# One softplus for the stick-breaking rows, softmax division on ScalarE, doubled queries in one GpSimd operation

## The chip, the core and the metric

The kernel runs on one core of one Trainium2 chip. A core has a matrix engine (TensorE, in the profile PE, with its weight loads as PEld), a vector engine (VectorE, DVE), an engine for activation functions (ScalarE, ACT), a general one (GpSimd, POOL) and one that issues transfers (SyncE, SP). Each works through its own list of instructions in order; semaphores tie the lists together. SBUF is the working memory, PSUM the memory that PE writes its results to, in banks of 128 rows by 512 fp32 columns.

The metric is device time in microseconds for one execution, as the median of several runs.

## The reference

One layer of a decoder on 1024 tokens of width 1024, in fp32: a norm, one input projection, three kinds of heads side by side, an output projection with a residual, and a squared-ReLU MLP with a residual. The change touches two of the three kinds of heads, each with six heads of width 64:

```python
def stick_breaking_attn(q, k, v):          # q, k: RMS-normed per head
    ...
    z = jnp.einsum('bhqd,bhsd->bhqs', qi, k) * scale
    mask = kpos[None, :] < qpos[:, None]
    log_1mb = jnp.where(mask, jax.nn.log_sigmoid(-z), 0.0)
    tail = lax.cumsum(log_1mb, axis=3, reverse=True) - log_1mb
    A = jnp.where(mask, jnp.exp(jnp.where(mask, jax.nn.log_sigmoid(z) + tail, 0.0)), 0.0)
    ...
def forgetting_attn(q, k, v, c):
    ...
    s = jnp.einsum('bhqd,bhsd->bhqs', qi, k) * scale + bias
    p = jax.nn.softmax(jnp.where(mask, s, NEG_BIG), axis=-1)
```

With sp(z) = ln(1 + exp(z)), the stick-breaking weight of a key is exp(z - S), where S is the sum of sp over this key and all later ones up to the query. So a row needs a softplus of each score, a running sum from the right, a subtraction and an exponential.

## The kernel before

The mixer part runs as eight units: six units m0 to m5, each with one stick-breaking head and one forgetting head, and two units of the recurrent heads (hg0, hg1), in the order m0, hg0, m1, m2, m3, hg1, m4, m5. While the core of one unit runs, the projection of the next (or, beside m5, the first part of the output projection) is laid between its steps, so that PE has matmuls whose inputs are ready. The steps are emitted by due times (`place`, with the tables SPAN and POW), and a scheduler then orders the instructions on each engine; that order is fixed when the program is built.

In `attn` a unit goes through 16 tiles of 128 queries (8 for each of its heads). A tile's keys come in one or two pieces of up to 512 columns; the widths are 128, 256, 384 or 512. That makes 12 pieces for each head and unit, 72 over the six units for each kind of head.

- `qprep` (L359) makes the queries ready, 256 at a time: POOL multiplies them by the per-token norm factor and writes them twice side by side (`qd`, L365, two operations), PE transposes them into PSUM (`qtp`, L369), ACT scales them by the gain and rounds (`qj`, L371), and DVE makes the remainder (L372). PE multiplies the pair with the keys.
- `qtile` (L375) makes the scores `z` in a PSUM bank (L396 to L399) and turns them into weights. Banks of the kind `z` are three, shared with `qtp` and some transposes.
- A stick-breaking piece (L401 to L416) is copied to SBUF by ACT (`zs`, L403). DVE takes the absolute value (L404), ACT makes exp and ln(1 + .) of it (L406, L407), DVE takes max(z, 0) (L409) and runs the scan from the right over both (L411). A subtraction (L414) runs on DVE in units 0, 2, 3, 4 and on POOL in 1 and 5, and ACT makes the last exponential (L415).
- A forgetting piece (L418 to L441) is read from PSUM by DVE, which takes off the bias and keeps the row maximum (L420); ACT makes the exponential with its row sum (L432), DVE the reciprocal of the sum (L437 or L439) and the product with it (L441).
- `back` (L444) transposes the weights on PE (L453) and evicts them (L457 on ACT, L459 on DVE); `av` (L465) multiplies them with the values (L472).

Several lines belong to helpers: L130 and L133 are the rounding and the remainder of `split`, which cuts an fp32 operand into two parts for the matmuls, and L173 to L175 are the three matmuls of `mm3`.

Per-token factors `qnr` are kept in five buffers, two of them taken by a unit. The rest of the program, from about 680 us on, is the second norm and the MLP, with one level of Strassen's scheme in each of its two products.

Of the kernel before, what the change touches and what calls it, by code (L numbers as in the profile page):

```python
# [18 lines left out]
P = 128  # L19
# [8 lines left out]
NEG = -1e30  # L28
C = 64
# [35 lines left out]
def hybrid_block(ctx, tc, x, lb_logits, norm1_g, w_in, hg_norm_g, sb_q_g, sb_k_g, fox_q_g, fox_k_g,  # L65
# [288 lines left out]
    def attn(name):  # L354
# [4 lines left out]
        def qprep(h, qq):  # L359
            half, q2 = divmod(qq, 2)  # L360
            gq = gq_fx if h else gq_sb
            ts = slice(q2 * 2, q2 * 2 + 2)
            qd = big("qd", "qd", [P, 2, 2, HD])
            for e in range(2):
                G.tensor_tensor(out=qd[:, :, e, :], in0=st["q"][half][:, ts, h, :],  # L365
                                in1=st["r"][half][:, ts, h:h + 1].broadcast_to([P, 2, HD]), op=ALU.mult)
            tp = pt("z", "qtp")[:, :256]
            for i in range(2):
                PE.transpose(out=tp[:, i * P:(i + 1) * P], in_=qd[:, i].rearrange("p e d -> p (e d)"), identity=ident)  # L369
            qj = big("qj", "qj", [P, 2, 256], F32R)  # L370
            S.activation(qj[:, 0], tp, AF.Copy, scale=gq)  # L371
            V.scalar_tensor_tensor(out=qj[:, 1], in0=tp, scalar=gq, in1=qj[:, 0], op0=ALU.mult, op1=ALU.subtract)  # L372
            cur["q", h, qq] = qj

        def qtile(h, i):  # L375
# [16 lines left out]
            for c, w in reversed(pcs):  # L392
# [7 lines left out]
                if sbk:  # L400
                    e = big("e", "sbe")[:, :w]  # L401
                    zs = big("zs", "sbz")[:, :w]
                    S.copy(zs, z)  # L403
                    V.tensor_scalar(out=e.bitcast(I32), in0=zs.bitcast(I32), scalar1=0x7fffffff, scalar2=None,  # L404
                                    op0=ALU.bitwise_and)
                    S.activation(e, e, AF.Exp, scale=-1.0)  # L406
                    S.activation(e, e, AF.Ln, bias=1.0)  # L407
                    r = big("r", "sbr")[:, :w]
                    V.tensor_scalar(out=r, in0=zs, scalar1=0.0, scalar2=None, op0=ALU.max)  # L409
                    rv = r[:, ::-1]  # L410
                    V.tensor_tensor_scan(out=rv, data0=rv, data1=e[:, ::-1], initial=0.0 if prev is None else prev,  # L411
                                         op0=ALU.add, op1=ALU.add)
# [11 lines left out]
            if not sbk:  # L424
# [15 lines left out]
                for c, w in pcs:  # L440
                    V.tensor_scalar(out=a_of[c], in0=a_of[c], scalar1=r, scalar2=None, op0=ALU.mult)  # L441
# [451 lines left out]
    V.memset(one_t, 1.0)  # L893

# [236 lines left out]
    PLACES = {"f_m": {"xo": (16, [P, 512]), "usum": (4, [P, 512]), "t1": (2, [P, 2, 512]), "ya": (3, [P, 2, 512]), "pad": (1, [P, 144])},  # L1131
# [176 lines left out]
```

## Time and profile before

| | |
|---|---|
| median of 3 runs | 1360.47 us (1359.05 to 1361.12) |
| the profiled execution | 1361.72 us |
| its span in the profile | 1360.0 us |
| PE busy | 1284.2 us, 94% |
| PE weight loads | 1064.6 us, 78% |
| DVE busy | 997.7 us, 73% |
| ACT busy | 707.4 us, 52% |
| POOL busy | 279.8 us, 21% |
| mean granted clock of PE | 0.979 of full speed |

A row of a group gives the line, the engine, the operation, the tile written and the tiles read, the shape, the count, then busy time in us and the mean of one in ns, then the time for which the engine stood idle just ahead of these instructions and what ended most of it. "(+3 forms)" says that several widths are in the group. PE's matmuls are pipelined and their ends are modelled, so a busy PE is not always PE at its peak. The chain of work that ended last is followed back from the last instruction: at each step to what released it, or to the instruction ahead of it on its engine.

### The profile page before, as it was taken

How to read it: one execution, taken by the hardware profiler on the slowest of the kernel's cores; microseconds unless marked ns; L12 is line 12 of the kernel's file. 1: busy time of each engine (PE TensorE's matmuls, PEld its weight loads, DVE VectorE, ACT ScalarE, POOL GpSimd, SP SyncE). 2: the span in 40 equal slices, each digit the busy share in tenths (PEclk: the TensorE clock that was granted, in tenths of full speed). 3: DMA queues.
4: the chain of work that ended last, by engine and by line, in shares of the span. 5: the costliest groups of instructions: out<-in, count | busy, mean ns of one | idle time of the engine just before them, and what ended most of it. 6: DMA issues, size and time to landing. Idle time of an engine off the chain costs nothing.

```text
span 1360.0 us, 19999 instructions
## 1 busy us (share of the span) xinstructions
PE 1284.2 (94%) x7200; PEld 1064.6 (78%) x7200; DVE 997.7 (73%) x1855; ACT 707.4 (52%) x1537; POOL 279.8 (21%) x342
## 2 busy tenths in 40 slices
PE   4999989989899899799897999999999899999998
PEld 4978878868688788467685888888887688888887
DVE  6758667877768668977669766666766898786865
ACT  5557344877688346765446554544454533333430
POOL 7112695432225764421100000000000000000000
PEclk9999998999999989799898999999999999999999
DMA  8200211200202020343453354344435973534322
GB/s 222 51 17 9 71 25 40 63 24 25 55 17 63 9 55 32 109 124 99 135 167 120 132 171 145 130 159 162 147 128 182 393 258 105 201 110 146 118 78 93
DMA packets 125931, 149.25 MB, mean 110 GB/s; under 512 B 46460, under 2 KB 73084, under 8 KB 125832
## 3 DMA queue, kind: packets, MB, share of 16 engines
q1 hardware_dynamic: 100464, 101.79, 24.6%
q10 hardware_dynamic: 25368, 46.17, 9.6%
q8 instruction: 57, 0.93, 0.3%
q14 instruction: 42, 0.34, 0.1%
HBM read 104.40 MB, written 43.54 MB: 109 GB/s over the span
## 4 chain that ended last, share of the span: by engine, by line
PE 75%; DVE 14%; ACT 4%; issue 2%; DMA 2%; POOL 2%; SPq 0%; ACTq 0%; POOLq 0%; DVEq 0%
PE pj L173 5%; PE pj L174 5%; PE pj L175 5%; PE av L472 3%; DVE sbr L411 3%; PE pc L1019 2%; PE pd L1018 2%; PE pc L1018 2%; PE pd L1019 2%; PE pd L1020 2%; PE pc L1199 2%; PE pc L1198 2%; PE pc L1020 2%; PE pc L1197 2%; PE pa L1018 2%
## 5 line engine op out<-in xcount | busy, mean ns | idle before, releaser
L173 PE MATMUL pj<-whi,hTh 128*128 128x384 f32 (+2 forms) x512 | 172.2, 339 | 2.2 <-ACT vg L619 1.2
L174 PE MATMUL pj<-wlo,hTh 128*128 128x384 f32 (+2 forms) x512 | 171.5, 336 | 0.0
L175 PE MATMUL pj<-whi,hTl 128*128 128x384 f32 (+2 forms) x512 | 170.9, 334 | 0.0
L130 ACT CAST fah<-ya 128x1024 fp32r<-128x1024 f32 x56 | 58.8, 1050 | 168.1 <-PE pd L1198 49.6
L173 PEld LDWEIGHTS pj<-whi,hTh 128*128 128x128 f32 x512 | 98.6, 193 | 5.9 <-ACT vg L619 1.5
L174 PEld LDWEIGHTS pj<-wlo,hTh 128*128 128x128 f32 x512 | 98.5, 192 | 2.5 <-issue 1.9
L175 PEld LDWEIGHTS pj<-whi,hTl 128*128 128x128 f32 x512 | 98.2, 192 | 2.3 <-issue 1.3
L411 DVE TENSOR_TENSOR_SCAN sbr<-sbr,sbe 128x128 f32<-128x128 f32 (+3 forms) x72 | 78.3, 1092 | 10.3 <-ACT sbe L407 9.6
L133 DVE TENSOR_TENSOR fal<-ya,fah 128x1024 fp32r<-128x1024 f32 x56 | 68.2, 1219 | 21.8 <-ACT fah L130 21.7
L365 POOL TENSOR_TENSOR qd<-qraw,qnr 128x128 f32<-128x128 f32 x96 | 47.8, 519 | 160.6 <-PE qtp L369 151.0
L472 PE MATMUL av<-at,vst 128*64 128x256 f32 x480 | 68.5, 368 | 1.6 <-ACT at L457 0.8
L133 POOL TENSOR_TENSOR wlo<-wraw,whi 128x384 fp32r<-128x384 f32 (+2 forms) x56 | 58.7, 1073 | 35.9 <-ACT whi L130 22.4
L457 ACT COPY at<-atp 128x128 f32<-128x128 f32 (+3 forms) x120 | 56.3, 479 | 10.5 <-PE atp L453 9.2
L133 DVE TENSOR_TENSOR fbl<-w2raw,fbh 128x1024 fp32r<-128x1024 f32 x48 | 58.2, 1215 | 1.6 <-ACT fbh L130 1.6
L173 PE MATMUL po<-woh,mTh 128*128 128x512 f32 x128 | 53.6, 418 | 4.8 <-DVE x L856 2.4
L397 PE MATMUL z<-kst,qj 128*128 128x512 f32 (+3 forms) x144 | 50.3, 374 | 7.1 <-DVE qj L372 7.1
L472 PEld LDWEIGHTS av<-at,vst 128*64 128x64 f32 x480 | 36.9, 137 | 25.6 <-issue 5.0
L396 PE MATMUL z<-kst,qj 128*128 128x512 f32 (+3 forms) x144 | 51.7, 384 | 4.0 <-ACT qj L371 3.6
L415 ACT ACTIVATE sbz<-sbz 128x128 f32<-128x128 f32 (+3 forms) x72 | 37.9, 529 | 30.2 <-DVE sbz L414 23.8
L432 ACT ACTIVATE fxa<-fxa,fxmn 128x512 f32<-128x512 f32 (+2 forms) x72 | 43.8, 612 | 18.8 <-DVE fxmn L427 9.8
L130 ACT CAST fbh<-w2raw 128x1024 fp32r<-128x1024 f32 x48 | 49.7, 1047 | 6.4 <-DMA w2raw<-in_w_ff_dram 5.1
L174 PE MATMUL po<-wol,mTh 128*128 128x512 f32 x128 | 52.1, 407 | 0.0
(355 smaller groups left out, 3786.9 us busy)
## 6 DMA issues: line engine op xcount, KB each, us to landing
w1raw<-in_w_ff_dram SPq DMA_DIRECT2D x32, 512.0 KB, 5.8
w2raw<-in_w_ff_dram SPq DMA_DIRECT2D x16, 1024.0 KB, 6.6
ya<-yd_s SPq DMA_DIRECT2D x32, 512.0 KB, 3.8
yd_s<-y ACTq DMA_DIRECT2D x48, 256.0 KB, 4.6
ya<-yd_a SPq DMA_DIRECT2D x24, 512.0 KB, 3.8
wraw<-in_w_in_dram SPq DMA_DIRECT2D x48, 192.0 KB, 3.3
wraw<-in_w_in_dram SPq DMA_DIRECT2D x16, 256.0 KB, 4.3
xraw<-in_x_dram SPq DMA_DIRECT2D x16, 256.0 KB, 3.4
```

The costliest lines, as they stand in the source:

```text
L130: S.copy(hi, raw)
L133: lo_eng.tensor_tensor(out=lo, in0=raw, in1=hi, op=ALU.subtract)
L173: PE.matmul(o, lhsT=lh, rhs=rh, start=start, stop=False)
L174: PE.matmul(o, lhsT=lh, rhs=rl, start=False, stop=False)
L175: PE.matmul(o, lhsT=ll, rhs=rh, start=False, stop=stop)
L396: PE.matmul(z, lhsT=qj[:, 0, qs], rhs=kst[:, :w], start=True, stop=False)
L411: V.tensor_tensor_scan(out=rv, data0=rv, data1=e[:, ::-1], initial=0.0 if prev is None else prev, op0=ALU.add, op1=ALU.add)
L457: S.copy(dst, tv)
L472: PE.matmul(o[h * HD:(h + 1) * HD, c0:], lhsT=st["v"][j // 4][:, j % 4, h, :], rhs=at[h][j // 4][:, j % 4, c0:], start=(j == 0), stop=(j = ...
L1018: PE.matmul(o, lhsT=wh[:, k], rhs=bh[:, k], start=start and k == 0, stop=False, **kw)
L1019: PE.matmul(o, lhsT=wh[:, k], rhs=bl[:, k], start=False, stop=False, **kw)
L1020: PE.matmul(o, lhsT=wl[:, k], rhs=bh[:, k], start=False, stop=k == 3, **kw)
```

## The change

```diff
+ZMAX = 40.0
...
+            q = st["q"][half][:, ts, h, :].unsqueeze(2).broadcast_to([P, 2, 2, HD])
             qd = big("qd", "qd", [P, 2, 2, HD])
-            for e in range(2):
-                G.tensor_tensor(out=qd[:, :, e, :], in0=st["q"][half][:, ts, h, :],
-                                in1=st["r"][half][:, ts, h:h + 1].broadcast_to([P, 2, HD]), op=ALU.mult)
+            if h:
+                G.tensor_tensor(out=qd, in0=q, op=ALU.mult,
+                                in1=st["r"][half][:, ts, h:h + 1].unsqueeze(3).broadcast_to([P, 2, 2, HD]))
+            else:
+                G.tensor_copy(qd, q)
...
                     zs = big("zs", "sbz")[:, :w]
-                    S.copy(zs, z)
-                    V.tensor_scalar(out=e.bitcast(I32), in0=zs.bitcast(I32), scalar1=0x7fffffff, scalar2=None,
-                                    op0=ALU.bitwise_and)
-                    S.activation(e, e, AF.Exp, scale=-1.0)
+                    V.tensor_scalar(out=zs, in0=z, scalar1=st["r"][i // 4][:, i % 4, 0:1], scalar2=ZMAX, op0=ALU.mult, op1=ALU.min)
+                    S.activation(e, zs, AF.Exp)
                     S.activation(e, e, AF.Ln, bias=1.0)
                     r = big("r", "sbr")[:, :w]
-                    V.tensor_scalar(out=r, in0=zs, scalar1=0.0, scalar2=None, op0=ALU.max)
-                    rv = r[:, ::-1]
-                    V.tensor_tensor_scan(out=rv, data0=rv, data1=e[:, ::-1], initial=0.0 if prev is None else prev,
-                                         op0=ALU.add, op1=ALU.add)
+                    V.tensor_tensor_scan(out=r[:, ::-1], data0=e[:, ::-1], data1=zero_t[:, 0:1].broadcast_to([P, w]),
+                                         initial=0.0 if prev is None else prev, op0=ALU.add, op1=ALU.add)
...
                 for c, w in pcs:
-                    V.tensor_scalar(out=a_of[c], in0=a_of[c], scalar1=r, scalar2=None, op0=ALU.mult)
+                    S.activation(a_of[c], a_of[c], AF.Copy, scale=r)
...
+    zero_t = const.tile([P, 1], F32, name="zero_t")
+    V.memset(zero_t, 0.0)
...
-    PLACES = {"f_m": {..., "pad": (1, [P, 144])},
+    PLACES = {"f_m": {..., "pad": (1, [P, 136])},
```

Four things change. The softplus is made in one branch: scores are bounded at 40, and ln(1 + exp(z)) is taken as it stands; absolute value, maximum and ACT's copy go, and the scan adds a zero that is repeated from one column. The norm factor of a stick-breaking query is no longer put into the query but into the same DVE operation that bounds the score, which reads PSUM. The division of the softmax goes from DVE to ACT. The doubled queries are written by one POOL operation, a plain copy for the stick-breaking head. A padding tile in the memory layout of the MLP is 8 columns narrower, beside the new constant of one column.

In numbers of instructions: DVE loses 144 (72 each of L404 and L409) and 72 (L441) and gains 72; ACT loses 72 copies and gains 72 products; POOL has 48 operations for queries where it had 96. PE's instructions and the transfers stay as many as they were. Since the scheduler works the whole program anew, other instructions move against each other too.

The first place is DVE's list in unit m4, at the two stick-breaking tiles with one and two pieces (`sbz` are scores, `sbe` the exponentials, `sbr` the running sums). Before:

```order
L404 TENSOR_SCALAR sbe<-sbz 128x128
L409 TENSOR_SCALAR sbr<-sbz 128x128
L404 TENSOR_SCALAR sbe<-sbz 128x512
L409 TENSOR_SCALAR sbr<-sbz 128x512
L411 SCALAR_TENSOR_TENSOR sbr<-sbr,sbe 128x128
L414 TENSOR_TENSOR sbz<-sbz,sbr 128x128
L411 SCALAR_TENSOR_TENSOR sbr<-sbr,sbe 128x512
L302 COPY vst<-pj 128x128
L414 TENSOR_TENSOR sbz<-sbz,sbr 128x512
```

And in the change, whose lines stand a little further down (its L409 is the new operation on PSUM, with `qnr` the norm factors, L413 the scan, L416 the subtraction):

```order
L409 TENSOR_SCALAR sbz<-z,qnr 128x128
L409 TENSOR_SCALAR sbz<-z,qnr 128x512
L413 SCALAR_TENSOR_TENSOR sbr<-sbe,zero_t 128x128
L416 TENSOR_TENSOR sbz<-sbz,sbr 128x128
L413 SCALAR_TENSOR_TENSOR sbr<-sbe,sbr,zero_t 128x512
L416 TENSOR_TENSOR sbz<-sbz,sbr 128x512
L409 TENSOR_SCALAR sbz<-z,qnr 128x256
```

Four operations ahead of the scans have become two; these read the bank `z` themselves, and the next piece's one stands behind two scans and two subtractions.

The second place is ACT's list in the same unit, where a forgetting tile's exponentials stand (`fxa` are its weights, `fxmn` the negated maximum, `mTh` the rounding of a part of the output projection's operand). Before:

```order
L432 ACTIVATE fxa,fxs<-fxa,fxmn 128x512
L432 ACTIVATE fxa,fxs<-fxa,fxmn 128x256
L406 ACTIVATE sbe<-sbe 128x384
L130 CAST mTh<-mraw 128x512
L406 ACTIVATE sbe<-sbe 128x512
L403 COPY sbz<-z 128x512
```

And in the change (L434 is the exponential, L443 the product with the reciprocal `fxr`, L410 and L411 the exp and ln of the softplus):

```order
L434 ACTIVATE fxa,fxs<-fxa,fxmn 128x512
L434 ACTIVATE fxa,fxs<-fxa,fxmn 128x256
L410 ACTIVATE sbe<-sbz 128x384
L138 ACTIVATE qnln<-qss,eps_t 128x16
L817 DMA mraw<-mix_m_1820 128x512
L443 ACTIVATE fxa<-fxa,fxr 128x512
L443 ACTIVATE fxa<-fxa,fxr 128x128
L131 CAST mTh<-mraw 128x512
L443 ACTIVATE fxa<-fxa,fxr 128x512
L443 ACTIVATE fxa<-fxa,fxr 128x256
L411 ACTIVATE sbe<-sbe 128x384
```

The products of two tiles now stand on ACT, ahead of the logarithm of a stick-breaking piece, and the copy from the bank has gone.

More of the change, by code (lines that the diff above doesn't have):

```diff
@@ L1129, in hybrid_block @@
     U = [None] * 4
-    PLACES = {"f_m": {"xo": (16, [P, 512]), "usum": (4, [P, 512]), "t1": (2, [P, 2, 512]), "ya": (3, [P, 2, 512]), "pad": (1, [P, 144])},
+    PLACES = {"f_m": {"xo": (16, [P, 512]), "usum": (4, [P, 512]), "t1": (2, [P, 2, 512]), "ya": (3, [P, 2, 512]), "pad": (1, [P, 136])},
               "f_hop": {"w2f": (1, [P, 2, D]), "yf": (2, [P, 2, 512]), "fof": (4, [P, 2, 512])},
```

## The prediction

> **What bounds the kernel now.** I read the page's first part, then busy time by stage (one window per unit), then the chain of work that ended last inside the stages with holes, and last the groups by line and by shape.
>
> ```profile
> span 1360.0 us, 19999 instructions
> 75.00:165.00 90.00, 86.19 (x575) 73.66 (x574) 65.67 (x157) 55.33 (x141) 27.91 (x35) 0.98 0.14 33
> 225.00:300.00 75.00, 70.99 (x445) 59.30 (x443) 62.02 (x157) 56.18 (x155) 31.20 (x36) 0.98 0.16 43
> 300.00:375.00 75.00, 70.87 (x404) 57.85 (x403) 55.03 (x125) 50.89 (x129) 17.82 (x22) 0.98 0.15 39
> 375.00:450.00 75.00, 75.00 (x539) 64.87 (x539) 52.81 (x120) 57.65 (x147) 26.66 (x31) 1.00 0.15 36
> 525.00:600.00 75.00, 62.28 (x349) 45.00 (x347) 65.76 (x143) 55.57 (x138) 30.52 (x37) 0.91 0.29 92
> 600.00:675.00 75.00, 69.05 (x357) 52.20 (x357) 50.08 (x111) 39.88 (x93) 11.60 (x12) 0.95 0.39 122
> 750.00:1360.00 610.00, 600.86 (x2623) 492.57 (x2621) 434.67 (x574) 256.94 (x357) 0.00 (x0) 1.00 0.47 159
> ```
>
> The columns are stretch, length, busy time of PE, weight loads, DVE, ACT and POOL, then the granted clock and the DMA share. From 750 us on PE is busy 600.86 of 610 us and nothing of the change runs there: that 45% of the span cannot move. The change lives in the six attention units, 75 to 675 us. There PE is full in 375 to 450 (75.00 of 75), so faster helpers gain nothing in that unit. It has holes in the others, the largest in 525 to 600: PE 62.28, weight loads only 45.00, DVE 65.76 of 75. So the question is what carries the chain in the stages with holes; the rows below are shares of 75 us, for 225, 300, 525 and 600 in turn.
>
> ```profile
> by line: DVE sbr L411 13.6%; issue 8.1%; ACT fxa L432 6.9%; PE av L472 5.7%; DVE sbe L404 4.4%; DVE fxa L420 3.9%; DMA wraw<-in_w_in_dram 3.6%; POOL qsq L311 3.5%; DVE qj L372 3.5%; DVE fxa L441 3.5%; DVE sbr L409 3.1%; PE atp L453 3.0%; AC
> by line: PE pj L173 14.8%; PE pj L174 13.8%; PE pj L175 13.7%; PE atp L453 8.2%; PE av L472 6.9%; DVE sbr L411 6.7%; DVE sbe L404 4.8%; PE z L397 4.1%; PE z L396 4.1%; DVE sbr L409 3.4%; DVE sbz L414 2.9%; DVE qsq L311 1.9%; PE qtp L369 1.8
> by line: DVE sbr L411 14.3%; DVE mTl L133 9.5%; PE av L472 7.1%; issue 6.5%; DVE sbz L414 6.2%; DVE fxa L441 5.1%; DVE sbr L409 4.4%; DVE kst L326 4.0%; PE pj L174 3.7%; DVE fxa L420 3.6%; DVE sbe L404 3.5%; PE pj L173 3.3%; PE pj L175 3.3%
> by line: PE po L173 14.0%; PE po L174 12.8%; PE po L175 12.7%; PE av L472 8.9%; PE atp L453 7.9%; DVE sbr L411 6.0%; issue 5.8%; DMA woraw<-in_w_out_dram 4.8%; DVE at L459 3.1%; DVE wol L133 2.7%; DVE fxa L420 2.6%; DVE sbr L409 2.3%; PE z
> ```
>
> The stick-breaking scan L411 leads the chain in two stages, and the three DVE operations that the change removes, L404, L409 and L441, stand on it beside the scan.
>
> **The change, part by part.**
>
> ```profile
> L404 DVE TENSOR_SCALAR sbe<-sbz 128x128 int32<-128x128 int32 (+3 forms) x72 | 32.2, 447 | 27.0 <-ACT sbz L403 26.6
> L409 DVE TENSOR_SCALAR sbr<-sbz 128x128 f32<-128x128 f32 (+3 forms) x72 | 31.2, 433 | 0.2
> L441 DVE TENSOR_SCALAR fxa<-fxa,fxr 128x512 f32<-128x512 f32 (+2 forms) x72 | 34.0, 503 | 0.9
> L403 ACT COPY sbz<-z 128x128 f32<-128x128 f32 (+3 forms) x72 | 33.6, 486 | 24.9 <-PE z L399 23.9 <-PE z L397 0.5
> L459 DVE COPY at<-atp 128x512 f32<-128x512 f32 (+3 forms) x24 | 13.2, 548 | 1.2 <-PE atp L453 1.2
> L420 DVE CUSTOM_DVE_ANT_0 fxa<-z,cb 128x128 f32<-128x128 f32 (+3 forms) x72 | 38.7, 549 | 12.3 <-PE z L399 11.7 <-PE z L397 0.2
> L372 DVE SCALAR_TENSOR_TENSOR qj<-qtp,gq_sb,qj 128x256 fp32r<-128x256 f32 x24 | 11.4, 474 | 0.8 <-ACT qj L371 0.6
> L459 DVE COPY at<-atp 128x256 f32<-128x256 f32 x4 | 1.7, 417 | 0.2 <-PE atp L453 0.2
> ```
>
> *Stick-breaking rows.* For 72 pieces ACT loses its copy L403 (33.6 us). DVE loses L404 and L409 (63.4 us) and gains one operation that reads PSUM with a per-row scalar. Its price is not in the trace. The floor is L404's 447 ns mean, as if PSUM cost nothing. L459 and L420 read PSUM at 548 and 549 ns over the same mix of widths. L372 reads PSUM with a per-row scalar too and takes 474 ns where the plain L459 copy of that width takes 417, 57 more. I take 549 + 57 = 606 ns, nearest to those rows: 43.6 us, between 32.2 and 43.6. So DVE sheds 63.4 - 43.6 = 19.8 us here, up to 31.2.
>
> ```profile
> 543.07 1.48 POOL L311 TENSOR_TENSOR qsq<-qraw 128x512 f32<-128x512 f32 x1
> 543.58 1.12 DVE L404 TENSOR_SCALAR sbe<-sbz 128x256 int32<-128x256 int32 x1
> 546.29 0.43 DVE L404 TENSOR_SCALAR sbe<-sbz 128x512 int32<-128x512 int32 x1
> 547.19 0.68 DVE L420 CUSTOM_DVE_ANT_0 fxa<-z,cb 128x512 f32<-128x512 f32 x1
> ```
>
> The saving lies in disturbed pieces. Undisturbed, L404 does 512 columns in 0.43 us and the PSUM reader L420 takes 0.68, so two for one gains little. While a POOL operation runs, L404 took 1.12 us for half the columns.
>
> The Trainium skill, "VectorE: DVE Perf Modes", section "Why PSUM operands drop a tier", speaks against this part: an fp32 operand in PSUM holds the operation to one element a cycle, where SBUF allows two. The undisturbed rows agree (0.68 against 0.43), and by them two for one saves 0.86 - 0.68 = 0.18 us a wide piece, 13 us over 72, against the 0.27 us a piece and 19.8 us that the means above, with POOL running, give; I keep the means.
>
> *The scan* keeps two operands, one now a repeated zero.
>
> ```profile
> L411 DVE TENSOR_TENSOR_SCAN sbr<-sbr,sbe 128x512 f32<-128x512 f32 x36 | 49.4, 1373 | 3.1 <-ACT sbe L407 2.9
> L411 DVE TENSOR_TENSOR_SCAN sbr<-sbr,sbe 128x128 f32<-128x128 f32 (+3 forms) x72 | 78.3, 1092 | 10.3 <-ACT sbe L407 9.6
> L588 DVE TENSOR_TENSOR_SCAN hb<-ht,ha 128x512 f32<-128x512 f32 x4 | 4.9, 1215 | 0.6 <-POOL ht L587 0.6
> ```
>
> A wide scan costs 1373 ns as now, or at best the 1215 of L588: 158/1373 of 78.3 us is 9 us, at most gained, or lost if the repeated operand were read slower. I take 0, since the order of the elements, both inputs from SBUF and the subtraction behind it stay.
>
> *Softmax division.* DVE sheds L441, 34.0 us; ACT gains 72 multiplications with a per-row scale.
>
> ```profile
> L432 ACT ACTIVATE fxa<-fxa,fxmn 128x512 f32<-128x512 f32 (+2 forms) x72 | 43.8, 612 | 18.8 <-DVE fxmn L427 9.8 <-DVE fxmn L429 8.2 <-DVE fxr L437 0.8
> L415 ACT ACTIVATE sbz<-sbz 128x128 f32<-128x128 f32 (+3 forms) x72 | 37.9, 529 | 30.2 <-DVE sbz L414 23.8 <-POOL sbz L414 5.8
> ```
>
> Same tile, same per-row pointer: 612 ns (L432), at least the 529 of L415 without one. So ACT gains 43.8 and loses 33.6: 10.2 us more, hidden in the fullest DVE stage, where ACT is busy 55.57 of 75. What stands bare is the new wait: ACT stops at each L441 in its order until DVE's reciprocal is done, and the next exponentials, evictions and casts queue behind it.
>
> The Trainium skill, "ScalarE: Activation LUTs", section "Rules for kernel authors", says to multiply on VectorE and not on ScalarE. The trace agrees on one operation alone: 612 against 503 ns. By it the sum would be that of rival 4 below.
>
> *Queries.* POOL issues 48 operations of 256 columns for 96 of 128, half of them plain copies.
>
> ```profile
> L365 POOL TENSOR_TENSOR qd<-qraw,qnr 128x128 f32<-128x128 f32 x96 | 47.8, 519 | 160.6 <-PE qtp L369 151.0 <-issue 9.6
> L675 POOL TENSOR_TENSOR hx<-hx,hf 128x256 f32<-128x256 f32 x24 | 22.4, 936 | 16.4 <-ACT hx L671 15.8
> PEld z L397 <- DVE qj L372: 9.3, 8, 2.4
> DVE sbe L404 <- ACT sbz L403: 26.6, 15, 5.0
> ```
>
> Two of 519 become one of at most 936 (L675); half a copy may halve it. POOL mostly waits here (160.6 us), so this alone is worth little: 8 waits of PE for qj, 0.1 to 0.5 us nearer each, 1 us at the low end. No DMA is added or moved.
>
> *Sum.* On the chain rows, L404 and L409 hold 3.3 + 2.3, 3.6 + 2.6, 3.3 + 2.6 and 1.7 us, 19.4 in all. The larger of the two in each stage over its mean gives 7.4 + 8.1 + 7.6 + 3.9 = 27 pieces, which come back at 606 ns: 16.4. Net -3.0. The 15 waits of DVE for the copy (last row above) lose one 486 ns step each, 7.3 us; I count half, the rest falling where PE is full or DVE has slack: -3.6. L441 holds 2.6 + 3.8 = 6.4 us, 13 pieces. Where DVE is the bound all of it goes, where the row's own delay is the bound it becomes 0.1 us longer; half and half: -2.5. Queries -1. Together **-10 us**. Behind this PE's own order is late next: PE idles 4.0, 4.1, 12.7 and 6.0 us in the four stages, so 27 us is about the most that filling them could give. I leave out 75 to 165, where PE idles 3.8 of 90.
>
> **The rivals.**
>
> ```profile
>   PEld z L396: 0.2, 1
> L414 DVE TENSOR_TENSOR sbz<-sbz,sbr 128x512 f32<-128x512 f32 x24 | 19.3, 803 | 0.3
> L404 DVE TENSOR_SCALAR sbe<-sbz 128x512 int32<-128x512 int32 (+3 forms) x13 | 6.1, 466 | 5.4 <-ACT sbz L403 5.4
> L409 DVE TENSOR_SCALAR sbr<-sbz 128x512 f32<-128x512 f32 (+3 forms) x13 | 6.4, 489 | 0.0
> L441 DVE TENSOR_SCALAR fxa<-fxa,fxr 128x512 f32<-128x512 f32 (+3 forms) x12 | 6.6, 574 | 0.2
> ```
>
> 1. *The scores' PSUM bank waits for DVE (slower).* Today ACT frees the three z banks; afterwards DVE does, in order, behind a scan and a subtraction. A PE that needs the bank then waits up to 1.373 + 0.803 = 2.18 us (L411 and L414, wide). The gain is eaten at five such waits; at seven of the 72, 15.3 - 10 = +5.3: 1367.0. For: DVE is the fullest helper in 525 to 600. Against: the forgetting heads' scores are already read from such a bank by DVE (L420), and under "who waited for it" the view of that line has one wait of PE, 0.2 us (first row). Chance 0.14.
> 2. *Hidden anyway.* PE takes over at once, as in 375 to 450, or a moved order opens as many holes as it closes: -1, 1360.7. Chance 0.14.
> 3. *DVE alone sets the stages.* The rows for 525 to 600 remove 6.1 + 6.4 + 6.6 = 19.1 us and bring back 13 x 0.606 = 7.9: -11.2 there. If 225 to 300, with a like DVE load, gives the same, -22: 1339.7. For: DVE 65.76 of 75. Against: PE idles only 4.0 us at 225. Chance 0.12.
> 4. *The division is on the delay path.* All 13 chain pieces of L441 lengthen by 0.1 us (612 - 503) instead of going: +1.4 in place of -2.5, so -6: 1355.7. For: ACT's L432, the operation just ahead, holds 6.9% of the chain at 225. Against: at 525 the chain has no ACT line among its first thirteen. Chance 0.10.
>
> **How the numbers follow.** The profiled run took 1361.72 us, span 1360.0 and 1.7 around it; the median of the runs is 1360.47, 1.25 less. Forecast: 1361.72 - 10 = 1351.7, or **1350.5** as a median, chance 0.50. The rivals' times are in the profile's terms too; less 1.25 they are 1365.8, 1359.5, 1338.5 and 1354.5. The range, 1337 to 1366, takes in all five and the cheaper scan's few microseconds on the chain. A measurement here tells about 0.2%, 2.7 us, from no change. Faster: 0.50 + 0.12 + 0.10 = 0.72; same 0.14; slower 0.14.
>
> **What would show it.** Right: DVE busy time falls by some 54 us (97.4 out, 43.6 in), ACT's rises by about 10, POOL's falls; the new line takes about 0.68 to 0.74 us for 512 columns and keeps that beside POOL; PE's idle time shrinks most in the unit of 525 to 600 and not at all in the one of 375. Wrong: PE waits for z banks whose reader is the new DVE line (rival 1); a stage as long as before with less DVE in it (rival 2); ACT idle before the multiplication, with the reciprocal as releaser, and PE's transposes waiting on it (rival 4); a scan of more than 1.4 us.

## The result, and the profile after

| | before | after |
|---|---|---|
| median of 5 runs | 1360.47 us (1355.44 to 1361.12) | 1368.95 us (1366.46 to 1371.53) |
| the profiled execution | 1361.72 us | 1366.46 us |
| its span | 1360.0 us | 1364.7 us |
| after to before | | 1.0071, 95% interval 1.0045 to 1.0096 |

The change made the kernel slower, by 8.5 us at the medians and 4.7 us between the two profiled executions. The forecast was 1350.5 us.

The page of after, its first part and its chain by engine:

```profile
span 1364.7 us, 19810 instructions
PE 1290.6 (95%) x7200; PEld 1066.1 (78%) x7200; DVE 979.0 (72%) x1712; ACT 715.6 (52%) x1537; POOL 261.5 (19%) x294
PE 83%; DVE 7%; ACT 4%; POOL 2%; issue 2%; DMA 1%; SPq 0%; ACTq 0%; POOLq 0%; DVEq 0%
```

DVE's share of the chain that ended last fell to 7%, from 14% on before's page. So the change took DVE off the chain, as it was meant to, and the kernel is slower all the same. The new operations and the scan, as groups by line (after has other line numbers: L409 is the bounded score, L413 the scan, whose second row is the pieces that carry on from another, L443 the product on ACT, L676 one step of the recurrent heads):

```profile
L409 DVE TENSOR_SCALAR sbz<-z,qnr 128x128 f32<-128x128 f32 (+3 forms) x72 | 42.6, 611 | 15.7 <-PE z L403 10.1 <-PE atp L455 4.7 <-PE z L401 0.5
L413 DVE TENSOR_TENSOR_SCAN sbr<-sbe,zero_t 128x128 f32<-128x128 f32 (+3 forms) x48 | 42.5, 894 | 14.8 <-ACT sbe L411 11.9 <-issue 1.1 <-POOL kraw L316 1.0
L413 DVE TENSOR_TENSOR_SCAN sbr<-sbe,sbr,zero_t 128x512 f32<-128x512 f32 x24 | 36.8, 1533 | 2.6 <-ACT sbe L411 2.4
L443 ACT ACTIVATE fxa<-fxa,fxr 128x512 f32<-128x512 f32 (+2 forms) x72 | 41.4, 609 | 5.8 <-DVE fxr L439 4.6 <-DVE fxr L441 1.1
L676 DVE TENSOR_TENSOR hxq<-hx,hq 64x256 f32<-64x256 f32 x24 | 29.0, 1251 | 2.7 <-PE hz L681 2.6
```

The prices were right: 611 ns for the new operation, 79.3 us for the scan (78.3 before), 609 ns for the product. The last row is not of the change: `hxq` cost 17.3 us before, with the same 24 operations. Busy time by stage, in the columns of the prediction's windows:

```profile
225.00:300.00 75.00, 72.24 (x453) 61.19 (x452) 56.26 (x126) 59.87 (x157) 26.23 (x27) 0.98 0.16 43
300.00:375.00 75.00, 74.00 (x443) 59.51 (x440) 48.22 (x112) 55.85 (x137) 15.53 (x15) 1.00 0.16 40
375.00:450.00 75.00, 73.66 (x522) 64.69 (x521) 53.39 (x97) 55.10 (x142) 31.83 (x34) 1.00 0.16 40
450.00:525.00 75.00, 62.94 (x650) 57.52 (x649) 62.00 (x103) 30.48 (x89) 41.06 (x42) 0.89 0.12 33
525.00:600.00 75.00, 64.88 (x357) 46.78 (x356) 61.23 (x124) 56.44 (x141) 29.77 (x31) 0.91 0.28 88
```

PE gained 1.25 us of busy time at 225, 3.13 at 300 and 2.60 at 525. It lost 6.64 in 450 to 525 (before's row there has PE at 69.58), the stage of the recurrent unit hg1. Milestones in the traces say the same. The last output of unit m3 is copied at 446.4 us, 5.8 earlier than before (452.2); the last of hg1 at 522.6, 2.4 later (520.2); the MLP's first matmul starts at 724.7, 3.0 later (721.7); the span ends 4.7 later. So the gain was there at 446 us, and was given back in hg1, in the last unit and in the MLP.

Where hg1 lost it, in the timeline of after (start, length, engine, line; in brackets the idle time of the engine just ahead and what ended it):

```profile
471.71 9.67 DVE L676 TENSOR_TENSOR hxq<-hx,hq 64x256 f32<-64x256 f32 x1
...
472.36 1.27 POOL L716 TENSOR_TENSOR hkd<-hkd,hf 128x512 f32<-128x512 f32 x1
473.59 1.26 POOL L725 TENSOR_TENSOR hb<-hb,hq 128x512 f32<-128x512 f32 x1
474.82 1.25 POOL L716 TENSOR_TENSOR hkd<-hkd,hf 128x512 f32<-128x512 f32 x1
476.04 1.25 POOL L725 TENSOR_TENSOR hb<-hb,hq 128x512 f32<-128x512 f32 x1
477.26 3.83 POOL L134 TENSOR_TENSOR wlo<-wraw,whi 128x384 fp32r<-128x384 f32 x4
...
481.52 1.23 PE L681 MATMUL hz<-hxq,hx 128*64 128x64 f32 x18 [8.48 <-DVE hxq L676]
```

One DVE operation, 0.42 us where it is undisturbed, took 9.67 us while POOL ran on to 481.09 without a pause; PE stood idle for 8.48 us until it was done. Two other kernels below with the same lists in hg1, x1_merge and x3_div, show 9.70 us each, so it is no chance of one execution.

### The profile page after: what moved, and what is told of

It reads as the page before. It is cut to its first block, busy times and chain, and to the rows that moved or that the text cites. A ratio compares the mean times of both kernels' runs of the same rounds, so it can differ in the third digit from the quotient of the medians.

```text
span 1364.7 us, 19810 instructions
## 1 busy us (share of the span) xinstructions
PE 1290.6 (95%) x7200; PEld 1066.1 (78%) x7200; DVE 979.0 (72%) x1712; ACT 715.6 (52%) x1537; POOL 261.5 (19%) x294
## 4 chain that ended last, share of the span: by engine, by line
PE 83%; DVE 7%; ACT 4%; POOL 2%; issue 2%; DMA 1%; SPq 0%; ACTq 0%; POOLq 0%; DVEq 0%
PE pj L174 7%; PE pj L176 6%; PE pj L175 6%; PE av L474 4%; PE atp L455 3%; PE pd L1201 2%; PE pc L1024 2%; PE pc L1023 2%; PE pc L1022 2%; PE pd L1022 2%; PE pd L1023 2%; PE pd L1024 2%; PE pc L1202 2%; PE pc L1203 2%; PE pc L1201 2%; PE pa L1022 2%
## 5 line engine op out<-in xcount | busy, mean ns | idle before, releaser
L474 PE MATMUL av<-at,vst 128*64 128x256 f32 x480 | 71.7, 383 | 2.0 <-DVE at L461 0.9
L409 DVE TENSOR_SCALAR sbz<-z,qnr 128x128 f32<-128x128 f32 (+3 forms) x72 | 42.6, 611 | 15.7 <-PE z L403 10.1
L413 DVE TENSOR_TENSOR_SCAN sbr<-sbe,zero_t 128x128 f32<-128x128 f32 (+3 forms) x48 | 42.5, 894 | 14.8 <-ACT sbe L411 11.9
L434 ACT ACTIVATE fxa<-fxa,fxmn 128x512 f32<-128x512 f32 (+2 forms) x72 | 43.8, 610 | 17.0 <-DVE fxmn L431 9.6
L1201 PE MATMUL pd<-fbh,fah 128*128 128x512 f32 x128 | 49.6, 400 | 2.2 <-ACT fbh L131 2.2
```

What stands on the lines that cost most here:

```text
L474: PE.matmul(o[h * HD:(h + 1) * HD, c0:], lhsT=st["v"][j // 4][:, j % 4, h, :], rhs=at[h][j // 4][:, j % 4, c0:], start=(j == 0), stop=(j = ...
L1201: PE.matmul(o, lhsT=lh[:, ts], rhs=rh, start=start and q == q0, stop=False, **kw)
```

## Experiments

Each experiment's ratio is to runs of before on the same chip. Three theories were set against each other: that the new **operations** cost what they save; that a **collision** and the **placement** of tiles took the gain; that the **order** that the scheduler finds anew decides.

### Placement, the collision, the tail

**x1_merge**: the change, with the zero put into the tile of ones, so that every later tile should keep before's address. In after, the new constant has moved the tiles between it and the padding; by how far is worked out from the padding, which gives up 8 columns of fp32 in exchange: 32 bytes in each row.

```diff
-    one_t = const.tile([P, 1], F32, name="one_t")
-    zero_t = const.tile([P, 1], F32, name="zero_t")
+    oz_t = const.tile([P, 4], F32, name="oz_t")
+    one_t, zero_t = oz_t[:, 0:1], oz_t[:, 1:2]
...
-    "pad": (1, [P, 136])
+    "pad": (1, [P, 144])
```

> The changed kernel with one edit: the new zero column lies in the tile of the ones, and the MLP's padding tile is 144 columns wide again, so that every later tile lies where it lay before the change. No engine's order changes. Theory (where the constant lies): the matmuls of the MLP's first product, 229.0 ns apart before and 231.9 after, go back to 229, and from 725 to 1050 us some 3 to 4 us go: ratio to the kernel before about 1.004. Rival (that spacing is chance of a run): spacing stays near 232 and the ratio at 1.007.

Measured 1364.76 us (1362.03 to 1370.77), ratio 1.0040 (1.0023 to 1.0057). PE's and POOL's lists are those of after, instruction by instruction, and DVE's but for the tile's name. **x5_shift** is the opposite: before with only the layout of the change, so that its instructions and their order are before's (one memset more, at the start).

> Before, with nothing but the changed kernel's memory layout: the unused one-column constant and the padding of 136 columns. Placement theory: the instructions and their order are those of before, but the matmuls of the MLP's first product, 760 to 1030 us, follow each other at about 232 ns instead of 229, so 3 to 4 us more: 1363.5 us, ratio 1.0025. Rival (placement costs nothing, the 4 us that the merged constant won came from the order): 229 ns and 1360.1 us.

Measured 1361.57 us (1360.57 to 1366.34), ratio 1.0015 (1.0000 to 1.0030). The windows view for the same 240 us of the MLP's first product (PE's matmuls are the first count), in before:

```profile
790.00:1030.00 240.00, 240.00 (x1050) 196.72 (x1049) 157.12 (x250) 121.82 (x201) 0.00 (x0) 1.00 0.45 152
```

In x5_shift:

```profile
790.00:1030.00 240.00, 240.00 (x1037) 194.12 (x1036) 154.90 (x245) 120.73 (x199) 0.00 (x0) 1.00 0.44 149
```

And in x1_merge:

```profile
790.00:1030.00 240.00, 240.00 (x1049) 196.74 (x1048) 158.42 (x252) 120.37 (x199) 0.00 (x0) 1.00 0.46 155
```

PE never idles, at full clock, yet it starts 1037 matmuls with the shifted tiles and 1050 or 1049 without: 13 matmuls of 0.231 us, 3.0 us in this stretch. After has 1037 too. From the MLP's first matmul to the end of the span it is 641.8 us in x5_shift against 638.2 in before, and 640.0 in after against 636.3 in x1_merge. So the cost of placement is shown by the traces, at 3 to 4 us in the MLP. The totals alone would not show it: they give 2 us (x5_shift, whose interval begins at 1.0000) to 4 us (after against x1_merge, whose intervals overlap). Why these addresses are slower for PE stays open.

**x2_gate**: x1_merge, and POOL held once in hg1, by an added copy of one element that waits for DVE's last `hxq`. In the trace it stands ahead of POOL's second product of `hkd`; DVE's list is that of x1_merge, and so is POOL's but for the copy.

```diff
                 S.activation(kd, kd, AF.Exp)
+                if pr == 1 and half == 0:
+                    G.tensor_copy(oz_t[HD:P, 2:3], st["xq"][1].rearrange("p (c h t) -> p c h t", h=2, t=32)[HD:P, HC, 1, 0:1])
                 G.tensor_tensor(out=kd, in0=kd, in1=k, op=ALU.mult)
```

> x1_merge and one more edit: in the second recurrent unit POOL copies one column that DVE's last query product wrote, between two of its own products, so POOL must pause until DVE is through. Theory (DVE gets no turn beside POOL's unbroken run): DVE's product of 9.67 us falls to under 3.5 us, PE's wait of 8.5 us for it to under 3, and 5 to 9 us go against x1_merge: ratio about 0.998 to 1.001. Rival (the hole is only where a general lateness shows): PE waits as long for something else in that stage and the time stays within 2 us of x1_merge.

Measured 1358.56 us (1355.74 to 1360.92), ratio 0.9998 (0.9983 to 1.0013), 6.2 us less than x1_merge on the same chip. PE's waits in 440 to 525 us (who waits, for whom, us in total, times, the longest) in x1_merge:

```profile
PE hz L681 <- DVE hxq L676: 11.9, 2, 8.4
```

And in x2_gate:

```profile
PE hz L681 <- DVE hxq L676: 5.8, 2, 3.5
```

The operation itself went from 9.70 to 3.43 us. It ended at 477.20, 0.28 us after POOL had come to the end of its `hb` (475.66 + 1.26) and stopped for the copy:

```profile
475.66 1.26 POOL L727 TENSOR_TENSOR hb<-hb,hq 128x512 f32<-128x512 f32 x1
477.68 0.19 POOL L717 COPY oz_t<-hxq 64x1 f32<-64x1 f32 x1 [0.75 <-DVE hxq L676]
```

So the collision is shown, at 6 us. Both repairs together bring the change back to before's time, and not below it.

**x3_div**: x1_merge with the division of the last unit back on DVE (`if pr == 5`), since in after the last 30 `av` matmuls of m5 take 5.22 us where before's took 3.45. **x4_all** has that and the gate.

> x1_merge and one more edit: in the last unit alone the softmax division is back on DVE. Theory (ACT's list is the bound at the end of the last unit): from the last scan to the end of the last weighted sum it was 12.0 us before and 17.1 us after; it falls to 12 to 14 us, and 3 to 5 us go against x1_merge: ratio about 1.000 to 1.002. Rival (the end of the unit is late for another reason, its order): under 1.5 us go.

> All three edits together: the constant's place, the pause of POOL, the division of the last unit on DVE. Theory (three separate places hold the loss, and the gain before 420 us is real): the parts add up, some 12 to 16 us under the changed kernel, ratio to the kernel before 0.995 to 0.998. Rival (the new operations cost time everywhere): ratio at or above 1.002.

Measured 1368.01 us, ratio 1.0055 (1.0036 to 1.0074), and 1357.80 us, ratio 0.9993 (0.9977 to 1.0010). Neither differs from its kernel without the edit, and x4_all lies between its theory (0.995 to 0.998) and its rival. The edit also moves other instructions of m5, so the order is not held here. The windows view of the end of m5 (655 to 675 us), where the granted clock is the number behind POOL's count, in before:

```profile
655.00:675.00 20.00, 14.96 (x78) 10.83 (x77) 10.15 (x27) 10.16 (x25) 1.29 (x1) 0.83 0.44 142
```

In after:

```profile
655.00:675.00 20.00, 12.26 (x64) 7.69 (x61) 6.71 (x20) 8.97 (x20) 1.28 (x1) 0.74 0.27 87
```

And in x3_div:

```profile
655.00:675.00 20.00, 13.95 (x63) 9.00 (x62) 8.21 (x25) 7.57 (x18) 1.10 (x1) 0.69 0.28 83
```

With the division back on DVE PE still idles there, and its clock is lower still. The last 30 `av` take 5.42 us in x3_div, and 5.41 in c4_nudge (below), which has before's own operations. The theory that the division makes the tail long has fallen.

### One part alone, one part undone

**p1_soft**, **p2_div** and **p3_query** are before with one part of the change each: the softplus with the query scale folded in; the division on ACT; one POOL operation for the doubled queries (a product for both kinds of heads).

```diff
-                    V.tensor_scalar(out=a_of[c], in0=a_of[c], scalar1=r, scalar2=None, op0=ALU.mult)
+                    S.activation(a_of[c], a_of[c], AF.Copy, scale=r)
```

This is all of p2_div. p3_query's is:

```diff
-            for e in range(2):
-                G.tensor_tensor(out=qd[:, :, e, :], in0=st["q"][half][:, ts, h, :],
-                                in1=st["r"][half][:, ts, h:h + 1].broadcast_to([P, 2, HD]), op=ALU.mult)
+            G.tensor_tensor(out=qd, in0=st["q"][half][:, ts, h, :].unsqueeze(2).broadcast_to([P, 2, 2, HD]), op=ALU.mult,
+                            in1=st["r"][half][:, ts, h:h + 1].unsqueeze(3).broadcast_to([P, 2, 2, HD]))
```

p1_soft has the lines of the change from `zs` to the scan, two plain copies in place of the two products for the stick-breaking queries, and x1_merge's tile for the zero.

> Before, with the softplus part alone (query scale folded in, POOL still with two operations, division on DVE, before's placement). Theory (this part carries the predicted gain, and what was lost lay in the collision with POOL and in placement): unit m3 ends 4 to 8 us earlier than before's 452.2 us, and the total is 1352 to 1359 us, unless its own order puts DVE beside an unbroken run of POOL in hg1 again, when 6 to 8 us of it go. Rival (the new PSUM operation or the scan costs what it saves): m3 ends where it did and the total is 1360 to 1366 us.

> Before, with the softmax division on ScalarE alone. Theory (it relieves an engine that is seldom the bound): 1357.5 to 1361 us, m3's end within 2 us of before's. Rival (ScalarE's order waits for the reciprocals and the transposes with it, the tail of m5 above all): 1363 to 1367 us, with the distance from the last scan to the second norm's first instruction longer than before's 23 us.

> Before, with the doubled queries in one GpSimd operation alone, a product for both kinds of heads. Theory: one operation of 256 columns in place of two of 128 saves GpSimd about 5 to 10 us of busy time and nothing of the span: 1358.5 to 1361.5 us. Rival (a longer single operation holds the second input port longer, so that VectorE's operations beside it stretch): 1362 to 1365 us.

| | us | ratio (95%) | last output of m3, us |
|---|---|---|---|
| p1_soft | 1353.77 | 0.9962 (0.9946 to 0.9978) | 440.3 |
| p2_div | 1394.35 | 1.0252 (1.0230 to 1.0275) | 464.4 |
| p3_query | 1373.46 | 1.0094 (1.0074 to 1.0113) | 456.4 |

The softplus alone is faster than both kernels: 3.75 us less than before on its chip. The division alone costs 37 us, the query operation 16, though POOL's busy time falls from 279.8 to 264.8 us by it. p2_div and p3_query lie outside both of their expectations, and where p3_query loses its 16 us was not told apart. Together the three would give +49 us; x1_merge has +4.7. The parts don't add.

p1_soft's gain is not less work for DVE in all: DVE is busy 997.6 us there and 997.7 in before, with 72 operations fewer. The exchange itself came out as priced (63.4 us of L404 and L409 became 42.6), but other operations took longer, the product L441 37.7 us where it had 34.0, and DVE's records overlap less. ACT is busy 681.7 us, 25.7 less.

**a1_nodiv** and **a2_twoq** undo one part of x1_merge: the division on DVE in all units; two query operations on POOL.

> The change, before's placement, with the division put back on VectorE in all units: softplus and the one query operation stay. Theory A (ScalarE's division is the dear part: alone it cost 34 us, and it is bearable in the change only because the softplus took 72 copies off ScalarE): faster than x1_merge's 1.0040 of before, ratio 0.994 to 0.999, 1349 to 1357 us. Theory B (what a part costs is mostly the order that the scheduler then finds, and not the operation): the ratio lies anywhere between 0.996 and 1.012, and VectorE waits again through a run of GpSimd in hg1 if the order puts them side by side.

> The change, before's placement, with two GpSimd operations for the doubled queries: softplus and the division on ScalarE stay. Theory A (the parts add): p3_query cost 16 us alone, so undoing it gives 1345 to 1350 us. Theory B (the order decides): no such gain, ratio 0.998 to 1.015, and the loss shows as a single VectorE operation of more than 5 us in hg1 or as PE's waits for fxa from ScalarE.

Measured 1359.40 us, ratio 1.0000 (0.9987 to 1.0012), and 1365.31 us, ratio 1.0043 (1.0028 to 1.0057). Undoing the query operation changes nothing against x1_merge's 1.0040, where alone it cost 0.94%. But the loss is not the same one: the longest `hxq` of a2_twoq is 2.36 us, so it is 0.45% behind x2_gate without the collision, and neither of the signs that its expectation named is there (PE waits 3.5 us for `fxa`, as in x1_merge). Undoing the division wins 0.4% against x1_merge, but nothing against x2_gate, and a1_nodiv has no `hxq` over 2 us: what it won is no more than the collision, and the division was not dear in the change.

**p2_gate** is p2_div with the same hold of POOL, as a second test of the collision.

> p2_div with GpSimd held once in hg1, as in x2_gate: an added one-element copy makes its second product wait for VectorE's last hxq. Theory (the same collision makes part of p2_div's 36 us: one hxq took 11.53 us there): that operation falls under 3 us, and the total by 7 to 11 us, to 1383 to 1388 us; the other 25 us are ScalarE's, which keeps its 72 copies beside the 72 products. Rival (the wait is hidden behind PE's other work): 1392 to 1396 us as before.

Measured 1380.78 us (1379.93 to 1385.06), ratio 1.0181 (1.0153 to 1.0209). The `hxq` in question, in p2_div's timeline:

```profile
493.30 11.53 DVE L674 TENSOR_TENSOR hxq<-hx,hq 64x256 f32<-64x256 f32 x1
```

And in p2_gate's:

```profile
493.84 3.01 DVE L674 TENSOR_TENSOR hxq<-hx,hq 64x256 f32<-64x256 f32 x1
```

PE's longest wait behind it, for a copy that comes after it on DVE's list, fell with it (460 to 560 us). In p2_div:

```profile
PE pj L173 <- DVE vst L302: 12.8, 2, 11.4
```

And in p2_gate:

```profile
PE pj L173 <- DVE vst L302: 4.6, 2, 3.2
```

Up to 518 us the lists of PE, DVE and ACT are the same in both kernels. The last DVE operation that is still in its old place, the first `hos`, starts at 517.95 in p2_gate and at 526.18 in p2_div, while ahead of the collision p2_gate was 0.5 us late. So the long operation cost 8 to 9 us here too, about the 0.7% between the two kernels. But it was not the hold that shortened it. POOL's list in p2_gate:

```profile
495.29 1.27 POOL L716 TENSOR_TENSOR hkd<-hkd,hf 128x512 f32<-128x512 f32 x1
496.53 1.44 POOL L725 TENSOR_TENSOR hb<-hb,hq 128x512 f32<-128x512 f32 x1
498.40 0.19 POOL L715 COPY oz_t<-hxq 64x1 f32<-64x1 f32 x1 [0.43 <-DVE hxq L674]
```

The operation ended at 496.85, 0.29 us after the end of `hkd` and more than a microsecond before POOL came to the hold. It got its turn at an end at which it had lost it in p2_div, and why is open. The 1.8% left are not told apart into ACT's extra work (742 us busy, before 707) and order.

### The order by itself

**c4_nudge** and **c5_nudge** are before with a one-column memset on POOL ahead of each pair of query operations (48), or ahead of each tile's transposes (96). No other operation is changed; the scheduler finds another order. POOL's busy time grows by 6.2 and 11.4 us.

```diff
+            G.memset(nudge, 0.0)
             qd = big("qd", "qd", [P, 2, 2, HD])
```

> Before with 48 one-column memsets on GpSimd, one ahead of each pair of query operations: no operation of before is changed or moved to another engine, but the scheduler finds another order (some 5 to 10 per cent of each engine's list moves). Theory A (operations decide): within 0.2 per cent of before, 1355 to 1360 us. Theory B (the order decides): off by 3 to 10 us, most likely up, since before's order was the one that its tables were set for.

> Before with a one-column memset on GpSimd ahead of each tile's transposes (96 in all): as c4_nudge, which cost 0.39 per cent with 48 of them at another place, no operation of before changed, another order. Theory (any other order of before's own operations costs some 0.2 to 0.5 per cent): ratio 1.002 to 1.006, 1362 to 1367 us. Rival (c4_nudge was one unlucky order): within 0.15 per cent, 1357 to 1361 us.

**x6_nudge** is x2_gate with c4_nudge's memsets: another order of the change.

> x2_gate (the change, before's placement, GpSimd held once in hg1; 0.9998 of before) with 48 one-column memsets ahead of the query operations: another order of the change's operations. Theory (the change was scheduled as it fell, so another order of it is as likely better as worse): ratio 0.995 to 1.006. Rival (orders of the change are all worse than before's tuned one, and its operations save less than an order costs): 1.001 to 1.006.

Measured: c4_nudge 1364.57 us, ratio 1.0039 (1.0024 to 1.0054); c5_nudge 1365.48 us, 1.0041 (1.0028 to 1.0054); x6_nudge 1357.13 us, 0.9974 (0.9961 to 0.9988). Windows of c4_nudge for the two units with the deepest holes:

```profile
525.00:600.00 75.00, 64.00 (x356) 47.25 (x354) 65.02 (x143) 54.74 (x136) 33.01 (x38) 0.89 0.29 91
600.00:675.00 75.00, 68.44 (x348) 50.58 (x346) 49.32 (x105) 37.61 (x86) 12.18 (x12) 0.91 0.35 106
```

And of x6_nudge:

```profile
525.00:600.00 75.00, 62.76 (x344) 44.06 (x342) 61.45 (x121) 55.28 (x134) 31.43 (x33) 0.91 0.33 102
600.00:675.00 75.00, 67.29 (x343) 50.32 (x342) 40.76 (x81) 35.78 (x81) 8.76 (x7) 0.93 0.38 117
```

Two other orders of before's own operations cost 5 to 6 us each, so a theory in which operations alone decide has fallen. A rival is that the memsets cost it themselves; against it, 96 cost no more than 48, and x6_nudge has the same 48 and is no slower than x2_gate. Another order of the repaired change is 3.5 us faster than before, and reaches the MLP at 716.0 us (before 721.7, x2_gate 720.2). In these windows c4_nudge's DVE is as full as before's (65.02 against 65.76), and the change's stays lower (61.45), but PE is no fuller for it there (62.76 against 64.00): the relief of DVE remains, and how much of it arrives changes with the order.

### How DVE lost its turn

**m1_beside**, **m2_beside**, **m3_apart** and **m4_likehg** leave out the whole layer and run DVE operations beside runs of POOL operations: in m1 the runs were drawn apart; in m2 they are held together, each operation writing the same tile; in m3 each writes a tile of its own, so that they overlap by 0.04 us, and a DVE operation is under way when the one under test starts; m4 repeats hg1's own row of operations eight times.

> Leaves out the whole layer: it runs one VectorE operation at a time, started after the first of a run of n GpSimd operations without a pause (n = 0, 3, 6, 12), and compares its length. Theory (VectorE waits for the port through the whole run): operations with two SBUF inputs, of 0.4 to 0.7 us alone, grow with n to about n times one GpSimd operation (12 of 128x384: 10 to 12 us), the one that reads PSUM doesn't grow. Rival (VectorE gets in after one GpSimd operation): at most 1.5 us longer, whatever n is.

> Leaves out the whole layer, as m1_beside, where the scheduler had drawn the GpSimd operations apart, so that only two or three stood beside each VectorE operation; here each run of n is held together. Theory (VectorE may lose its turn at every boundary of an unbroken run): among the operations with two SBUF inputs some take more than two GpSimd operations, over 2 us and up to 10 with n = 12; the one that reads PSUM stays at 0.75 us. Rival (VectorE always gets in after the GpSimd operation under way, as in m1_beside): none is over 2.0 us beside its length alone, whatever n is, and the 9.67 us of hg1 needs something more than a long run.

> Leaves out the whole layer, as m2_beside. There GpSimd's operations wrote one tile in turn and stood 0.08 us apart; in hg1 they overlap by 0.03 us (one starts at 473.593, the one before ends at 473.624). Here each of a run writes a tile of its own, and the operation under test starts behind another of VectorE, in the middle of a GpSimd operation. Theory (VectorE gets its turn in the gap between two GpSimd operations, and loses it where they overlap): with n = 12 operations with two SBUF inputs last over 2 us, some up to the end of the run, 10 to 12 us; the one that reads PSUM stays at 0.75. Rival (a gap makes no difference): none is over 1.5 us longer than with n = 0.

> Leaves out the whole layer: the row of operations of hg1 by itself, eight times: GpSimd runs two products of 256 columns, two of 64 rows, four in place on 128x512 and four of 128x384 without a pause, VectorE a short operation of 32 to 480 columns (it shifts the rest in time), two subtractions of 128x512 with a repeated column and two products of 64x256 on the other 64 rows. Theory (it is these operations, 64 rows beside 64 rows or results in place, that make VectorE lose its turn): some of the sixteen 64x256 products take over 2.4 us, up to 10. Rival (it takes the rest of the kernel, ScalarE and the matmuls, or a moment that is rarely met): all of them stay under 1.6 us, as in m3_apart.

From m3_apart's timeline, a 64x256 product without a run of POOL operations (n0; POOL then has only operations of one column) and beside a run of twelve (n12), a SBUF to SBUF operation, one that reads PSUM, and a scan with a zero repeated from one column, each with n0 and n12:

```profile
43.80 0.41 DVE L90 TENSOR_TENSOR half1n0w384q<-g,a 64x256 f32<-64x256 f32 x1
57.29 1.21 DVE L90 TENSOR_TENSOR half1n12w384q<-g,a 64x256 f32<-64x256 f32 x1
102.04 0.48 DVE L94 TENSOR_SCALAR tsn0w384q<-g,half 128x512 f32<-128x512 f32 x1
115.51 1.22 DVE L94 TENSOR_SCALAR tsn12w384q<-g,half 128x512 f32<-128x512 f32 x1
130.75 0.74 DVE L96 TENSOR_SCALAR psn0w384q<-z,g 128x512 f32<-128x512 f32 x1
143.78 0.74 DVE L96 TENSOR_SCALAR psn12w384q<-z,g 128x512 f32<-128x512 f32 x1
189.70 1.22 DVE L98 TENSOR_TENSOR_SCAN scanzn0w384q<-g,zero 128x512 f32<-128x512 f32 x1
204.58 2.01 DVE L98 TENSOR_TENSOR_SCAN scanzn12w384q<-g,zero 128x512 f32<-128x512 f32 x1
```

Beside POOL an operation from SBUF is 0.7 to 0.8 us longer, whether 6 or 12 POOL operations stand there, and the one from PSUM not at all. In all four kernels DVE got in behind the POOL operation under way: none was more than 1.1 us longer than alone, and that one stood beside operations of 1.26. m4's 64x256 products took 1.05 and 0.41 us. So neither a long run, nor overlapping POOL operations, nor hg1's own row is enough. The sixteen traces of the whole kernel have 384 `hxq` on DVE. During 257 of them one POOL operation ended, during 25 two or three, during 96 none. Only six saw more, in two orders of hg1: 9 ends each in after, x1_merge and x3_div; 11 in p2_div, and 7 in an earlier operation of 5.93 us that p2_div and p2_gate have both. So it is rare. That a pause of POOL lets DVE in is shown by x2_gate, and seen again in x4_all and x6_nudge, which have the same hold (3.45 and 3.46 us); by what the turn is lost in the whole kernel stays open.

The Trainium skill, "SBUF — State Buffer", section "SBUF: two separate sides", calls the port pair of the two engines an exclusive lock, held for the whole of an instruction by whichever starts first. The small kernels agree (0.41 us becomes 1.21); the 9.67 us, past nine POOL operations, is more than that rule gives.

## Why the prediction was wrong

- **The prices held.** 611 ns against 606 for the PSUM operation, 609 against 612 for the product, the scan unchanged (79.3 us against 78.3; m3_apart has 1.22 us for 512 columns with the repeated zero, and as much with a full second operand). POOL fell by 18.3 us, ACT rose by 8.2 (10 forecast). For the operation on PSUM it was right to keep the means with POOL running: undisturbed it takes 0.74 us where one from SBUF takes 0.48, but beside POOL it stays at 0.74 and the other becomes 1.22.
- **The chain moved as forecast.** L413 leads the chain in none of the four stages any more, and m3 ends 5.8 us earlier in after, 11.9 in p1_soft. As forecast PE's idle time did not shrink at 375 (it grew by 1.3), and it shrank by 2.6 us at 525; but it shrank most at 300, by 3.1. At 525 the chain is now led by "issue" (13.2%) and, behind `av`, by POOL's `woh` and `wol` (9.0% and 8.7%), the two parts of the output projection's weights, where the scan led before.
- **The step that failed: the sum took the rest of the program as it stood.** "The change lives in the six attention units" left hg1 out, and "that 45% of the span cannot move" was said of the MLP, which is full and has none of the change's operations. The first lost 6 us by the collision, the second some 3 us by 32 bytes of placement, in a part of the diff (the constant and the padding) to which the prediction gave no price.
- **A second error lies in "DVE busy time falls by some 54 us".** It fell by 18.7. The busy times of groups were added as if nothing else on DVE would change. Of the 35 us between, 11.7 are `hxq`; the rest is other operations that took longer and records that overlap less. p1_soft shows the same without the long `hxq`: 19.8 us of relief were forecast for its part, and DVE's busy time fell by 0.1, yet the kernel was faster. So the share of the gain that comes from DVE, from ACT's missing copy and from the shorter row was not separated.
- **The -10 us supposed before's order.** Before's own operations in two other orders cost 1.0039 and 1.0041; the repaired change in two orders costs 0.9998 and 0.9974. By this comparison the change saves 0.4 to 0.7%, 6 to 9 us, so the size may have been nearly right. It is not shown: four orders are few, the change's two were repaired by hand where before's two were not, and a2_twoq, the change less its query part, has 1.0043 without the collision. Against before's one good order 0 to 3.5 us are left.
- **The rivals.** Rival 1 (z banks wait for DVE) was seen and was small: PE waited 1.9 us in 3 waits for L409, where seven waits were priced at 15.3. Rival 4 (division on the delay path) likewise, as the waits of after between 75 and 680 us show:

```profile
PE hz L681 <- DVE hxq L676: 12.0, 2, 8.5
PE z L400 <- ACT qj L375: 4.6, 5, 1.5
...
PE atp L455 <- ACT fxa L443: 3.4, 3, 1.9
...
PE z L400 <- DVE sbz L409: 1.9, 3, 1.1
```

- The first row is the wait that counted, and no rival named it, though the prediction quoted DVE at 1.12 us beside POOL and knew that all lists are ordered anew. The nearest was rival 2, "a moved order opens as many holes as it closes": x2_gate landed on it at 0.9998. That the times agree does not prove it: the holes that closed and opened were not matched one by one.
- The Trainium skill, "ScalarE: Activation LUTs", section "Rules for kernel authors", would leave the multiplication on VectorE. The runs agree in part: moved to ACT alone, with ACT still copying, it cost 1.8 to 2.5% (p2_gate, p2_div; part of it order); in the change, whose softplus had freed ACT, a1_nodiv's 1.0000 against x2_gate's 0.9998 shows nothing to gain by the rule.
- Left open: the tail. In 655 to 675 us the clock is lower in other orders too (0.74 in x2_gate, 0.66 in a1_nodiv, which divides on DVE, 0.67 in c5_nudge, before's own operations) and 0.83, as in before, in x6_nudge, which divides on ACT. So it is no matter of the division; what before's order does better there was not tried.

## What to carry to other kernels

Where a scheduler orders the whole program anew, price an edit against a control that changes the order and nothing else (here 0.4%), before a few us are put down to an operation. Look beyond the edited lines for what the new order puts side by side, above all a DVE operation with two SBUF operands beside an unbroken row of POOL operations, and try to hold POOL with one waiting instruction if PE stands behind it; x2_gate won 6 us by it. Put a new constant into an existing tile, so that nothing else moves.

## What was not expected of the hardware

- One DVE operation of 0.42 us took 9.67 and 11.53 us beside POOL, in the whole kernel only.
- A shift of tiles, by 32 bytes as worked out from the padding, slowed a full PE at full clock from 1050 to 1037 matmuls in 240 us.
- A scan whose second operand is one repeated column costs the same 1.22 us as one with two full operands, and is lengthened by POOL to the same 2.01.
